# Folding a state scaling into its update, and turning one score matmul round, in a hybrid decoder step

## The chip, the cores and the metric

The kernel runs on one core of a Trainium2 chip. The metric is the device time of one execution in microseconds (us); lower is better. The engines named below are TensorE (PE, with its weight loads PEld), VectorE (DVE), ScalarE (ACT), GpSimd (POOL) and SyncE (SP), which issues most of the transfers.

## The reference

One inference step of one decoder layer, for a prompt of 512 tokens and for a sample group of 8 sequences with 4 new tokens each, with shared weights. Two parts matter here.

The sample group's mLSTM carries a state C (value x key, 128 x 128) for each of 8 sequences b and 4 heads h. With one chunk of 4 tokens the new state is

```python
m_new = jnp.maximum(btot + m, jnp.max(dec, axis=1))
w_s = jnp.exp(dec - m_new[:, None, :])
w_c = jnp.exp(btot + m - m_new)
C_new = w_c[..., None, None] * C + jnp.einsum('bsh,bshe,bshd->bhed', w_s, vi, ki)
```

The prompt's compressed attention compares each of 8 query heads (4 for each of 2 key heads) with 32 compressed key blocks:

```python
s_c = jnp.einsum('bkgqd,bkcd->bkgqc', qi, kc) - slopes * d_c
p_c = masked_softmax(s_c, d_c >= 0)
o_c = jnp.einsum('bkgqc,bkcd->bkgqd', p_c, vc)
```

Everything is float32; the large matmuls are made of three products of split halves.

## The kernel before

The layer is written as Python generators that yield after each small step. `weave(bg, fg)` runs a background generator and lets a foreground one advance in proportion to the numbers that both yield. The stretch that matters is the two `weave(compress(kv), fg)` calls. The background, `compress(kv)`, is the sample group's key and value compression: 8 sequences of 4 steps each, every step a gathered tile turned on VectorE (L1193), summed on GpSimd (L1195), split into two halves on ScalarE and VectorE (L213, L214), and multiplied on TensorE (L218 to L220 into the banks `bd` and `xa`). At the end of a sequence, a tile `cur` is copied to `nxt` with one row's shift by two transfers (L1301, L1302), which line L1330 then reads. The foreground is a chain: the prompt's mLSTM (`mlstm`), with the prompt's compressed scores (`cmp_prompt`, called `cb`) advanced on every second step, then the sample's mLSTM (`mlstm_s`), then the sample's attention (`sample`), which can't begin before `compress(1)` has its weights.

The order written so is only a priority. A planner with a model of the engines' timing then fixes the order of instructions on each engine and each transfer queue, so an edit can move instructions that it doesn't touch. Every queue runs in its order: an instruction that waits holds up what stands behind it. `tc.issue_after` and `tc.keep_in_program_order` pin a few places.

Matmul results go to 8 PSUM banks: `ptp` has two of them ("tp" in the profile), `psp` and `ppo` one each ("sp", "po"). A float32 matmul shows as two records for each call.

In `cmp_prompt`, `kb` holds 32 keys of each key head v, laid out twice along the 128 partitions. For each block i of 128 query tokens, 8 matmuls (L1359) load a 128 x 128 slice of the queries `Q2` as weights and stream the 32 keys; the result has queries on the partitions. Two VectorE adds (L1362) bring in the bias `CB`, and a softmax over 32 keys follows on VectorE, GpSimd and ScalarE (L1366 to L1375). The probabilities are turned back by two transposes (L1382).

In `mlstm_s`, the state lies in two tiles `C0[c]`, each of 4 sequences by 4 heads by 128. Once TensorE has read a tile (transposes L1058, products L1065), GpSimd multiplies all of it by the factors `wcb` (L1070, two instructions of 128 x 2048). Then `outer(h, kz)` makes the outer products of 4 sequences in one PSUM bank (L1100) and VectorE adds that bank to the state (L1101, 8 instructions of 128 x 512). The state goes out in 8 transfers (L1118).

The tile `vcn` (128 x 1024) is a scratch space before it is a result: `compress` loads a quarter of its first-layer weights into it (`vr`, L588), for the keys at the beginning and for the values again after `mlstm` is done in program order (in `produce`, at the earliest).

Of the kernel before, what the change touches and what calls it, by code (L numbers as in the profile page):

```python
# [6 lines left out]
F32 = mybir.dt.float32  # L7
# [3 lines left out]
AF = mybir.ActivationFunctionType  # L11
OP = mybir.AluOpType
# [24 lines left out]
def body(tc, I, O, stage=99, dbg=None):  # L37
    nc = tc.nc
    with ExitStack() as top:
        def pool(name, bufs=1, side="left", stack=None, space=None):  # L40
            kw = dict(name=name, bufs=bufs)
            if space is not None:
                kw["space"] = space
            else:
                kw["side"] = side
                kw["reuse_waits"] = "tile"
            return (stack or top).enter_context(tc.tile_pool(**kw))

        ptp = pool("ptp", 2, space=PSUM)
        psp = pool("psp", 1, space=PSUM)  # L50
# [6 lines left out]
        def bank(p):  # L57
            if p is pxb:
                return rot(pxa, pxc)
            return p.tile([128, 512], F32, name=p_names[id(p)])  # L60
# [4 lines left out]
        def rot(*pools):  # L65
            key = tuple(id(p) for p in pools)
            turn[key] = turn.get(key, -1) + 1
            return bank(pools[turn[key] % len(pools)])
# [8 lines left out]
        def push(name, **kw):  # L77
            st = ExitStack()
            right[name] = st
            return pool(name, stack=st, **kw)  # L80
# [28 lines left out]
        Q2 = qp.tile([128, 8, 512], R32, name="Q2")  # L109
# [41 lines left out]
        ident = const.tile([128, 128], F32, name="ident")  # L151
# [51 lines left out]
        def evac(out, in_, scale=None):  # L203
            flip[0] = (flip[0] + 1) % flip[1]
            if flip[0]:
                nc.scalar.activation(out, in_, AF.Copy, scale=1.0 if scale is None else scale)
            elif scale is None:
                nc.vector.tensor_copy(out, in_)
            else:
                nc.vector.tensor_scalar(out, in_, scale, None, op0=OP.mult)  # L210
# [180 lines left out]
        for c in range(3):  # L391
            c0 = 512 + 264 * c
            dense_N(w0 if c == 0 else w12(c), 264,
                    lambda i, c=c: [((kvn[:, i] if i < 4 else kvs)[:, c * 264:c * 264 + 264], 0, 264)], (pbd, pxb))
# [167 lines left out]
        p = bank(ptp)  # L562
# [170 lines left out]
        vcn = cs.tile([128, 8, 128], F32, name="vcn")  # L733
# [10 lines left out]
        def need(x):  # L744
            while x not in done:
                yield 1
# [201 lines left out]
        def mlstm_s():  # L948
            mw = push("mls", side="right")
            C0 = [mw.tile([128, 4, 4, 128], F32, name=f"C0{c}") for c in range(2)]  # L950
            for b in range(8):
# [13 lines left out]
                                    op=OP.subtract)  # L965
# [23 lines left out]
            p = bank(ptp)  # L989
# [24 lines left out]
            p = bank(ptp)  # L1014
# [6 lines left out]
            p = bank(ptp)  # L1021
            for h in range(4):
                nc.tensor.matmul(p[:, 8 * h:8 * h + 8], sel[:, h], wc, start=True, stop=True)
            wcb = mw.tile([128, 8, 4], F32, name="wcb")
            nc.vector.tensor_copy(wcb.rearrange("p b h -> p h b"), p[:, :32].rearrange("p (h b) -> p h b", h=4))
            p = bank(psp)
# [7 lines left out]
            p = bank(ptp)  # L1034
# [16 lines left out]
            for c in range(5):  # L1051
                if c < 4:
                    CT = CTs[c] = mw.tile([128, 8, 129], F32, name="CT", bufs=2)
                    nc.vector.tensor_copy(CT[:, :, 128], n0T[:, 8 * c:8 * c + 8])
                    for b in (2 * c, 2 * c + 1):
                        p = bank(ptp)
                        for h in range(4):
                            nc.tensor.transpose(p[:, 128 * h:128 * h + 128], C0[b // 4][:, b % 4, h], ident)  # L1058
                        q = 4 * (b % 2)
                        evac(CT[:, q:q + 4, 0:128], p.rearrange("p (h e) -> p h e", h=4))  # L1060
                if c > 0:
                    CT = CTs.pop(c - 1)
                    for b in (2 * c - 2, 2 * c - 1):
                        for h in range(4):
                            nc.tensor.matmul(pn[32 * h:32 * h + 32, 0:129], Qz[:, h, 32 * b:32 * b + 32],  # L1065
                                             CT[:, 4 * (b % 2) + h], start=False, stop=b == 7)
                if c == 2 or c == 4:
                    cc = C0[c // 2 - 1]
                    b0 = 2 * c - 4
                    nc.gpsimd.tensor_tensor(cc, cc, wcb[:, b0:b0 + 4, :, None].to_broadcast([128, 4, 4, 128]), op=OP.mult)  # L1070
                yield
            pe_ = bank(psp)
            for h in range(4):
# [15 lines left out]
            p = bank(psp)  # L1089
            for h in range(4):  # L1090
# [3 lines left out]
                                               op0=OP.mult, op1=OP.add)  # L1094
            nc.sync.dma_start(O[S_N][0].rearrange("b h d -> b (h d)"), nsn)

            def outer(h, kz):
                for c in range(2):
                    p = bank(ptp)
                    nc.tensor.matmul(p, W3[:, h], kz[:, 4 * c:4 * c + 4], start=True, stop=True)  # L1100
                    nc.vector.tensor_tensor(C0[c][:, :, h], C0[c][:, :, h], p.rearrange("p (b d) -> p b d", b=4), op=OP.add)  # L1101

            kzs = {}
            for h in range(5):
# [7 lines left out]
            p = bank(ptp)  # L1112
            nc.tensor.transpose(p[:, :128], hs_, ident)
            for h in range(4):
                nc.vector.scalar_tensor_tensor(oF[:, 4 + h, 512:], p[:, 32 * h:32 * h + 32], gm[:, h:h + 1], sgs[:, h],
                                               op0=OP.mult, op1=OP.mult)
# [224 lines left out]
        def cmp_prompt():  # L1341
            yield from need(("p", 0))
            pk_ = push("cmps", side="right")
            with tc.issue_after(cgs["ml"]["pool"].ins):
                CB = cmp_consts(pk_)
            kb = pk_.tile([128, 2, 32], F32, name="kb")
            for v in range(2):
                for w in range(2):
                    nc.vector.tensor_copy(kb[64 * w:64 * w + 64, v], kcP[64 * v:64 * v + 64])
            yield  # L1350
            pend = {}
            for i in range(5):
                if i < 4:
                    sb = pk_.tile([128, 8, 32], F32, name="csb", bufs=2)
                    S = bank(psp)
                    for j in range(4):
                        for v in range(2):
                            c0 = j * 64 + v * 32
                            nc.tensor.matmul(S[:, c0:c0 + 32], Q2[:, 4 * v + j, 128 * i:128 * i + 128].bitcast(F32), kb[:, v],  # L1359
                                             start=True, stop=True)  # L1360
                    for v in range(2):
                        nc.vector.tensor_tensor(sb[:, 4 * v:4 * v + 4],  # L1362
                                                S[:, :256].rearrange("p (h v s) -> p v h s", h=4, v=2)[:, v],
                                                CB[:, i, 4 * v:4 * v + 4], op=OP.add)
                    mn = pk_.tile([128, 8], F32, name="cmn", bufs=2)
                    nc.vector.tensor_reduce(mn, sb, axis=AX.X, op=OP.min)  # L1366
                    nc.vector.tensor_scalar(mn, mn, 0.1 * BIG, None, op0=OP.min)
                    nc.gpsimd.tensor_tensor(sb, sb, mn[:, :, None].to_broadcast([128, 8, 32]), op=OP.subtract)
                    nc.scalar.activation(sb, sb, AF.Exp, scale=-1.0)
                    sm_ = pk_.tile([128, 8], F32, name="csm", bufs=2)  # L1370
                    nc.vector.tensor_reduce(sm_, sb, axis=AX.X, op=OP.add)
                    nc.vector.tensor_scalar(sm_, sm_, 1e-30, None, op0=OP.max)
                    nc.vector.reciprocal(sm_, sm_)
                    nc.vector.tensor_tensor(sm_, gat[:, i, 0:24:3], sm_, op=OP.mult)
                    nc.gpsimd.tensor_tensor(sb, sb, sm_[:, :, None].to_broadcast([128, 8, 32]), op=OP.mult)  # L1375
                    pend[i] = sb
                    yield
                if i > 0:
                    sb = pend.pop(i - 1)
                    p = bank(ptp)  # L1380
                    for v in range(2):
                        nc.tensor.transpose(p[:, 128 * v:128 * v + 128], sb[:, 4 * v:4 * v + 4], ident)  # L1382
                    nc.scalar.activation(PcT[:, :, 128 * i - 128:128 * i], p[:, :256].rearrange("p (v t) -> p v t", v=2), AF.Copy)
                yield
# [413 lines left out]
        def front():  # L1798
            cb = cgs["cb"] = cmp_prompt()
            n = 0  # L1800
            for x in mlstm():
                yield x
                n += 1
                if ("p", 0) in done and n % 2 == 0:
                    next(cb, None)

        fg = chain(paced(front(), 1.3), paced(mlstm_s(), 2), paced(sample(), .8), open_late())
        flip[1] = 4
        burst(fg, 8)
# [131 lines left out]
        for i in range(2):  # L1941
            x = cw.tile([128, D], F32, name="PTx", bufs=2)
# [365 lines left out]
        for kind, i in order:  # L2308
# [5 lines left out]
            else:  # L2314
                c0, m = parts[i]
# [238 lines left out]
        for hf in (1, 0):  # L2554
            for j in range(8):
                p = rot(*dbk)
# [24 lines left out]
```

## Time and profile before

| | |
|---|---|
| time, median of 3 runs | 1245.95 us (1245.32 to 1247.04) |
| the profiled execution, its own time | 1257.88 us |
| its span in the profile | 1256.2 us |
| granted TensorE clock, mean | 0.97 |
| TensorE matmul, busy | 1174.9 us (94%) |
| VectorE, busy | 867.2 us (69%) |
| ScalarE, busy | 628.6 us (50%) |
| GpSimd, busy | 583.9 us (46%) |

The profile shows one execution. Times in it count from the start of the span. Busy shares are means over stages that differ much; what matters is the stretch in which the changed lines run, from about 290 to 430 us. A matmul's end is modelled, and back-to-back records overlap, so a run of records is best read by its first start and last end.

### The profile page before, as it was taken

The page shows a single profiled execution, that of the slowest core. Times are in us where ns is not written, and L with a number is a line of the kernel's source. Part 1 is how long each engine was busy: PE and PEld are TensorE (multiplying, and loading weights), DVE is VectorE, ACT ScalarE, POOL GpSimd, SP SyncE. Part 2 cuts the span into 40 slices and gives each one's busy share as a digit, 9 for nine tenths or more (in the row PEclk, how much of TensorE's full clock was granted, in tenths as well). Part 3 has the DMA queues.
Part 4 walks back from the last instruction along what each step waited for, and adds up shares of the span by engine and source line. Part 5 has one row for each costly group of instructions (what it writes and reads, how often), then busy time and mean ns, then how long its engine had stood idle before and what let it go on. Part 6 is the DMA issues. An engine that isn't in the chain of part 4 may idle for free.

```text
span 1256.2 us, 24868 instructions
## 1 busy us (share of the span) xinstructions
PE 1174.9 (94%) x9388; PEld 1078.2 (86%) x9388; DVE 867.2 (69%) x1881; ACT 628.6 (50%) x1424; POOL 583.9 (46%) x696
## 2 busy tenths in 40 slices
PE   7999999889998779998989998999999999999996
PEld 5998999588986677876889987589899999999996
DVE  6336674577886876776556576544988878888874
ACT  5235666755546525567533333433565555465452
POOL 1013354577664854744234100034786486486443
PEclk9999999899888899999989999999999999999998
DMA  7324240132142464567659399750023322422411
GB/s 231 100 53 105 83 151 3 52 115 76 59 133 92 124 212 147 174 208 236 160 156 179 101 217 280 258 168 1 1 92 108 104 93 79 133 93 77 135 52 72
DMA packets 141771, 154.33 MB, mean 123 GB/s; under 512 B 17449, under 2 KB 123689, under 8 KB 141394
## 3 DMA queue, kind: packets, MB, share of 16 engines
q1 hardware_dynamic: 131922, 119.17, 31.9%
q0 software_dynamic: 9728, 33.56, 8.3%
q8 instruction: 74, 1.21, 0.4%
q14 instruction: 47, 0.39, 0.1%
HBM read 141.67 MB, written 13.12 MB: 123 GB/s over the span
## 4 chain that ended last, share of the span: by engine, by line
PE 72%; DVE 12%; issue 5%; DMA 3%; ACT 3%; POOL 2%; SPq 2%; another core or an unknown queue 0%; DVEq 0%; POOLq 0%; ACTq 0%
PE bd L218 7%; PE bd L220 7%; PE xc L2255 7%; PE xa L2255 7%; PE bd L219 6%; PE bd L2255 5%; PE tp L2255 5%; PE xa L219 2%; PE xa L218 2%; PE xa L220 2%; DVE sp L2195 2%; PE tp L634 1%; PE xc L219 1%; PE xc L218 1%; PE xc L220 1%
## 5 line engine op out<-in xcount | busy, mean ns | idle before, releaser
L214 POOL TENSOR_TENSOR al<-fraw,ah 128x512 fp32r<-128x512 f32 (+1 forms) x104 | 127.3, 1226 | 152.7 <-ACT ah L213 124.2
L214 DVE TENSOR_TENSOR wlo<-wraw,whi 128x1024 fp32r<-128x1024 f32 (+3 forms) x74 | 76.4, 1061 | 27.6 <-ACT whi L213 27.4
L213 ACT ACTIVATE whi<-wraw 128x1024 fp32r<-128x1024 f32 (+3 forms) x74 | 62.9, 890 | 64.7 <-DMA wraw<-in_w_xv 28.8
L218 PE MATMUL bd<-w1h,xh 128*128 128x256 f32 x256 | 78.8, 309 | 6.6 <-ACT xh L213 5.1
L213 ACT ACTIVATE ah<-fraw 128x512 fp32r<-128x512 f32 (+1 forms) x112 | 65.8, 593 | 37.8 <-PE xc L2255 11.7
L220 PE MATMUL bd<-w1h,xl 128*128 128x256 f32 x256 | 78.7, 313 | 6.3 <-DVE xl L214 6.3
L213 ACT ACTIVATE xh<-xf 128x768 fp32r<-128x768 f32 x64 | 53.5, 842 | 52.6 <-POOL xf L1195 30.7
L1195 POOL TENSOR_TENSOR xf<-xf 128x256 f32<-128x256 f32 x64 | 52.9, 834 | 56.6 <-DVE xf L1193 38.0
L219 PE MATMUL bd<-w1l,xh 128*128 128x256 f32 x256 | 76.1, 298 | 0.0
L214 DVE TENSOR_TENSOR xl<-xf,xh 128x768 fp32r<-128x768 f32 x64 | 62.9, 987 | 15.1 <-ACT xh L213 13.7
L625 POOL TENSOR_SCALAR sb<-sb,rs,gat 128x128 f32<-128x128 f32 (+3 forms) x64 | 45.9, 722 | 54.3 <-DVE rs L624 40.2
L218 PEld LDWEIGHTS bd<-w1h,xh 128*128 128x128 f32 x256 | 51.9, 203 | 11.2 <-ACT xh L213 7.1
L213 ACT ACTIVATE ah<-sp 128x512 fp32r<-128x512 f32 (+1 forms) x64 | 35.5, 555 | 50.3 <-DVE sp L2195 26.6
L220 PEld LDWEIGHTS bd<-w1h,xl 128*128 128x128 f32 x256 | 51.2, 202 | 10.6 <-DVE xl L214 7.6
L219 PEld LDWEIGHTS bd<-w1l,xh 128*128 128x128 f32 x256 | 52.0, 203 | 1.4 <-issue 0.9
L219 PE MATMUL bd<-hlo,whi 128*128 128x272 f32 x176 | 52.0, 296 | 0.0
L218 PE MATMUL bd<-hhi,whi 128*128 128x272 f32 x176 | 51.7, 294 | 0.0
L220 PE MATMUL bd<-hhi,wlo 128*128 128x272 f32 x176 | 51.4, 292 | 0.0
L2195 DVE TENSOR_TENSOR sp<-fraw 128x512 f32<-128x512 f32 (+1 forms) x32 | 47.9, 1497 | 0.2
L214 DVE TENSOR_TENSOR al<-sp,ah 128x512 fp32r<-128x512 f32 (+1 forms) x64 | 40.8, 637 | 9.7 <-ACT ah L213 8.5
L1869 POOL TENSOR_TENSOR acc<-acc,sq 128x272 f32<-128x272 f32 x35 | 31.3, 895 | 34.3 <-ACT sq L1868 33.9
L220 PE MATMUL bd<-hh,wlo 128*128 128x272 f32 x160 | 46.6, 292 | 0.0
(998 smaller groups left out, 4830.4 us busy)
## 6 DMA issues: line engine op xcount, KB each, us to landing
fraw<-in_w_gate SPq DMA_DIRECT2D x11, 1024.0 KB
fraw<-in_w_up SPq DMA_DIRECT2D x11, 1024.0 KB
fraw<-in_w_down SPq DMA_DIRECT2D x24, 384.0 KB
mkv<-in_cache_mem_k SPq DMA_DIRECT2D x64, 128.0 KB
mkv<-in_cache_mem_v SPq DMA_DIRECT2D x16, 512.0 KB
wraw<-in_w_in SPq DMA_DIRECT2D x8, 512.0 KB
wraw<-in_w_xq SPq DMA_DIRECT2D x4, 1024.0 KB
wraw<-in_w_xk SPq DMA_DIRECT2D x4, 1024.0 KB
```

The costliest lines, as they stand in the source:

```text
L213: nc.scalar.activation(hi, src, AF.Copy)
L214: (eng or nc.gpsimd).tensor_tensor(lo, src, hi, op=OP.subtract)
L218: nc.tensor.matmul(out, ah, bh, start=first, stop=False, **kw)
L219: nc.tensor.matmul(out, ah, bl, start=False, stop=False, **kw)
L220: nc.tensor.matmul(out, al, bh, start=False, stop=last, **kw)
L625: (nc.vector, nc.gpsimd)[1].tensor_scalar(sb[:, :n], sb[:, :n], rs, gat[:, i, 3 * h + 1 + br:3 * h + 2 + br], op0=OP.mult, op1=OP.mult)
L634: ins = nc.tensor.transpose(p[:, 128 * k:128 * k + 128], sb[:, 128 * k:128 * k + 128], ident)
L1195: nc.gpsimd.tensor_tensor(xf[:, :, 128:192], xf[:, :, 0:64], xf[:, :, 64:128], op=OP.add)
L1869: nc.gpsimd.tensor_tensor(acc[hf], acc[hf], sq, op=OP.add)
L2195: nc.vector.tensor_tensor(o, a, b, op=op)
L2255: nc.tensor.matmul(p[:, :HALF], w[a][:, k], x[b_][:, k], start=first and k == 0 and i == 0, stop=last and k == n - 1 and i == 2, skip_grou ...
```

## The change

Two edits that don't touch each other.

The sample's state: the two GpSimd multiplications are gone. In `outer`, each of the 8 additions of a bank to the state becomes 4 VectorE instructions, one for each sequence b, that compute state times its factor plus the product (`scalar_tensor_tensor`, 128 x 128, factor read as one value per partition, product read from PSUM): 32 instructions in all.

The prompt's compressed scores: the keys become the weights (32 columns) and all 512 query tokens are streamed past them. For each key head v, the 4 query heads j go to the 4 groups of 32 PSUM partitions of one bank, and ScalarE copies that bank to SBUF, into a view `ST` of the tile `vcn`. In the loop over i, two TensorE transposes bring 128 tokens into the old layout, and one VectorE add over all 8 heads takes the place of two. The generator yields once more.

```diff
@@ mlstm_s
-                if c == 2 or c == 4:
-                    cc = C0[c // 2 - 1]
-                    b0 = 2 * c - 4
-                    nc.gpsimd.tensor_tensor(cc, cc, wcb[:, b0:b0 + 4, :, None].to_broadcast([128, 4, 4, 128]), op=OP.mult)
                 yield
@@ outer
                     nc.tensor.matmul(p, W3[:, h], kz[:, 4 * c:4 * c + 4], start=True, stop=True)
-                    nc.vector.tensor_tensor(C0[c][:, :, h], C0[c][:, :, h], p.rearrange("p (b d) -> p b d", b=4), op=OP.add)
+                    for b in range(4):
+                        x = C0[c][:, b, h]
+                        nc.vector.scalar_tensor_tensor(x, x, wcb[:, 4 * c + b, h:h + 1], p[:, 128 * b:128 * b + 128],
+                                                       op0=OP.mult, op1=OP.add)
@@ cmp_prompt
             pend = {}
+            ST = vcn.rearrange("p (v c) o -> p v (c o)", v=2)
+            for v in range(2):
+                S = bank(psp)
+                for j in range(4):
+                    nc.tensor.matmul(S[32 * j:32 * j + 32], kb[:, v], Q2[:, 4 * v + j].bitcast(F32), start=True, stop=True)
+                nc.scalar.activation(ST[:, v], S, AF.Copy)
+            yield
             for i in range(5):
                 if i < 4:
                     sb = pk_.tile([128, 8, 32], F32, name="csb", bufs=2)
                     S = bank(psp)
-                    for j in range(4):
-                        for v in range(2):
-                            c0 = j * 64 + v * 32
-                            nc.tensor.matmul(S[:, c0:c0 + 32], Q2[:, 4 * v + j, 128 * i:128 * i + 128].bitcast(F32), kb[:, v],
-                                             start=True, stop=True)
                     for v in range(2):
-                        nc.vector.tensor_tensor(sb[:, 4 * v:4 * v + 4],
-                                                S[:, :256].rearrange("p (h v s) -> p v h s", h=4, v=2)[:, v],
-                                                CB[:, i, 4 * v:4 * v + 4], op=OP.add)
+                        nc.tensor.transpose(S[:, 128 * v:128 * v + 128], ST[:, v, 128 * i:128 * i + 128], ident)
+                    nc.vector.tensor_tensor(sb, S[:, :256].rearrange("p (h s) -> p h s", h=8), CB[:, i], op=OP.add)
```

## Rows read from the trace of the kernel before

**Rows 1.** Stretches of 20 us: busy us of each engine, granted clock, DMA.
```profile
320.00:340.00 20.00, 20.00 (x163) 19.11 (x162) 17.66 (x39) 12.88 (x33) 13.65 (x15) 0.91 0.20 60
...
400.00:420.00 20.00, 14.97 (x111) 12.37 (x112) 18.45 (x24) 12.10 (x30) 16.68 (x11) 0.80 0.20 61
```

**Rows 2.** Chain of work that ended last, 280 to 460 us: start, us, what.
```profile
316.00 3.05 PE sp L1359 x16
...
348.70 1.71 PE sp L1359 x16
...
355.05 0.59 PE sp L1359 x6
...
412.48 3.48 DVE dns L1078
```

**Rows 3.** Timeline around the two GpSimd multiplications: start, us, engine.
```profile
395.11 3.61 POOL L1070 TENSOR_TENSOR C<-C,wcb 128x2048 f32<-128x2048 f32 x1 [5.26 <-PE tp L1058]
...
396.55 3.25 DVE L214 TENSOR_TENSOR w1l<-wr,w1h 128x1024 fp32r<-128x1024 f32 x1
...
407.28 1.23 DVE L214 TENSOR_TENSOR w1l<-wr,w1h 128x1024 fp32r<-128x1024 f32 x1 [1.39 <-ACT w1h L213]
...
411.34 4.60 POOL L1070 TENSOR_TENSOR C<-C,wcb 128x2048 f32<-128x2048 f32 x1
...
412.40 3.56 DVE L1078 TENSOR_TENSOR dns<-dns 128x1 f32<-128x1 f32 x1
...
415.91 1.27 POOL L214 TENSOR_TENSOR wsl<-wr,wsh 128x512 fp32r<-128x512 f32 x1
...
416.51 0.64 DVE L1101 TENSOR_TENSOR C<-C,tp 128x512 f32<-128x512 f32 x1
417.08 0.14 DVE L1079 RECIPROCAL dns<-dns 128x1 f32<-128x1 f32 x1
...
417.21 0.79 PE L1100 MATMUL tp<-kz,W 96*128 96x512 f32 x1 [3.67 <-DVE C L1101]
```

**Rows 4.** Groups by line and shape, 308 to 360 us: count, busy us, mean ns.
```profile
L1359 PE MATMUL sp<-kb,Q 128*128 128x32 f32 x64 | 8.9, 292 | 1.4 <-DVE csb L1362 1.1 <-issue 0.2
...
L1362 DVE TENSOR_TENSOR csb<-sp,CB 128x128 f32<-128x128 f32 x8 | 1.9, 279 | 0.9 <-PE sp L1359 0.9
```

**Rows 5.** Timeline, stand-ins for the new TensorE and ScalarE work: start, us, engine.
```profile
353.80 0.41 PE L1382 MATMUL tp<-ident,csb 128*128 128x128 f32 x2
...
408.27 0.43 PE L1065 MATMUL po<-CT,Qz 128*32 128x129 f32 x8
...
463.13 0.58 ACT L206 ACTIVATE kt<-tp 128x512 f32<-128x512 f32 x1
...
602.71 1.07 PE L1522 MATMUL sp<-kt,Qn 128*32 128x512 f32 x8
```

**Rows 6.** Loads into vcn on SP's queue, a copy to nxt, and their readers.
```profile
L588 SPq DMA_DIRECT2D vcn<-in_cmp_w_v x4: 529/546/551, 251.5 to 259.7; - x4
...
347.84 0.53 SPq L1301 DMA_DIRECT2D nxt<-cur  x1
...
409.64 1.06 ACT L213 ACTIVATE w1h<-vcn 128x1024 fp32r<-128x1024 f32 x1 [0.65 <-PE bd L220]
```

**Rows 7.** Durations min/median/max ns, first and last start, of VectorE's state additions and a look-alike.
```profile
L1101 DVE TENSOR_TENSOR C<-C,tp x8: 643/681/690, 409.2 to 425.8; 128x512 f32<-128x512 f32 x8
...
L1093 DVE SCALAR_TENSOR_TENSOR nsn<-n,wN,sp x4: 327/331/334, 385.8 to 399.7; 8x128 f32<-8x128 f32 x4
```

**Rows 8.** Timeline, back-to-back VectorE instructions of one line.
```profile
419.55 1.27 DVE L1101 TENSOR_TENSOR C<-C,tp 128x512 f32<-128x512 f32 x2
...
429.98 0.72 DVE L1115 SCALAR_TENSOR_TENSOR oF<-tp,cv,sgs 128x32 f32<-128x32 f32 x4
```

**Rows 9.** Chain of work, one float32 matmul of 512 columns (two records).
```profile
284.55 0.86 PE tp L799 x2
```

**Rows 10.** The 4 us after 416 us, columns as in rows 1.
```profile
416.00:420.00 4.00, 2.79 (x12) 2.70 (x13) 3.96 (x8) 1.96 (x8) 4.00 (x3) 0.50 0.12 33
```

## The prediction

> **What bounds the kernel now.** I read the page first: TensorE is busy for 94% of the span (the table above), so the question is whether the changed lines run where TensorE sets the pace. The table of 20 us stretches [rows 1] shows two different answers. From 320 to 340 us TensorE is busy all 20 us, with VectorE close behind at 17.66; there a shorter matmul list should shorten the kernel until VectorE takes over. From 400 to 420 us TensorE is busy only 14.97 us and VectorE 18.45; there VectorE sets the pace, and TensorE time is worth little.
>
> Next I read the chain of work that ended last [rows 2]. The score matmuls of L1359 stand in it five times, from 316.00 to 355.05 us; the five pieces add up to 6.3 us (3.05 + 1.71 + 0.59 + 0.37 + 0.59; the middle two of the small ones are not shown). Further on it holds one piece of 3.48 us on a VectorE instruction that handles one number per partition. That is far too long for such an instruction, and the timeline around the GpSimd multiplications explains it [rows 3]. The first multiplication runs from 395.11 to 398.72 us. A VectorE split that starts at 396.55 takes 3.25 us, where the next of the same shape takes 1.23. The second runs from 411.34 to 415.94 us; the tiny L1078 starts at 412.40 and ends at 415.96, at the same moment, where the equally small L1079 takes 0.14. So these two GpSimd instructions hold VectorE, and TensorE then sits idle for 3.67 us until VectorE has freed a bank.
>
> **The scores, part by part.** Removed: 64 records of L1359, 8.9 us of TensorE [rows 4]. The first 16 of them end just before TensorE stalls for other reasons and are not in the chain, so 6.3 us are on the path [rows 2].
>
> Added on TensorE: two runs of 4 calls with 32-column weights and 512 streamed columns. The nearest row is the sample's score matmul of exactly that form, 8 records in 1.07 us [rows 5]; two are 2.1 us. Then 4 pairs of transposes, each like the pair of L1382 at 0.41 us [rows 5]: 1.6 us. TensorE saves 8.9 - 3.7 = 5.2 us.
>
> On the path the first pair of runs takes the place of the block that was off it, about as long, so nothing changes there. Each later block becomes a pair of transposes: -6.3 + 1.6 = -4.7 us. VectorE has 2.3 us of slack in each 20 us of that stretch [rows 1], and the stretch is 40 us long, so 4.6 us is about all that it lets through. The hand-over is new too: bank `psp` is single, and the second run must wait until ScalarE has copied the first out. Such a copy takes 0.58 us [rows 5], and ScalarE is busy for 12.88 of 20 us [rows 1], so some of that shows. I take -3.5 us. Bounds: nothing gained if VectorE already paces the stretch, -5.2 if all TensorE time counts.
>
> Two VectorE adds of 0.28 us [rows 4] become one of twice the width for each i; I count that at nothing. The extra yield moves the foreground chain one step later; it is hidden by the chain's own wait, since the sample's attention can't start before `compress(1)` has its weights. Without that cover it would cost about one step's share of the weave, which the planner's freedom blurs anyway, and I leave it to the range.
>
> Moved: the tile `vcn` now holds the scores. The four loads of the value weights into it were issued from 251.5 to 259.7 us [rows 6], long before the scores. They now have to wait until the last scores have been turned, near where L1359 ends today (355 us [rows 2]). Their reader starts at 409.64 us [rows 6], so some 50 us are left for four loads of 0.55 us of queue time each: nothing, as long as they don't stand in front of something urgent on SP's queue. That is a rival below.
>
> **The state, part by part.** Removed: 8.2 us of GpSimd, which alone is worth nothing, and the hold on VectorE: 3.25 - 1.23 = 2.0 us and 3.56 - 0.14 = 3.4 us, together -5.4 us [rows 3].
>
> Added: 8 additions go, 32 narrower instructions come. The look-alike is L1093, the same operation with one operand in PSUM and 128 elements, 0.331 us; an addition of 512 takes 0.681 [rows 7]. By durations that is 32 x 0.331 - 8 x 0.681 = 10.6 - 5.4 = +5.1 us. Back to back, instructions overlap a little: two additions take 1.27 us, so a second one costs 0.59; four 32-wide ones take 0.72, or 0.18 each [rows 8]. Between these, 128 elements cost about 0.25 us (an estimate by a straight line), and the sum is 32 x 0.25 - 8 x 0.59 = +3.3 us. I take +4.0, between the two, since the four of one bank run back to back and then wait for the next.
>
> Would GpSimd's other work hold the new instructions as well? The addition at 416.51 us, with one operand in PSUM, took 0.64 us under a GpSimd split that ran from 415.91 to 417.18 [rows 3], so I take it that it doesn't. Net: -5.4 + 4.0 = -1.4 us. Bounds: -5.4 if the additions hide in VectorE's gaps, +5.1 if the holds were not on the path.
>
> [...]
>
> **The sum.** -3.5 - 1.4 = -4.9 us on the profiled execution's own 1257.88 us, that is 1253.0, or 0.39% less. The median of the runs shown is 1245.95, nearly 1% below the profiled one; the same share of it gives 1241.1 us. A difference of 0.2%, 2.5 us, is about what a measurement of this kernel can tell from no change, so "faster" is below 1243.5 and "slower" above 1248.4.
>
> **The rivals.** First, nothing arrives, because VectorE paces both places. For it: 17.66 and 18.45 of 20 us [rows 1]. The TensorE gain becomes waiting for VectorE (0), and the state costs its durations' sum (-5.4 + 5.1 = -0.3): about 1245.6 us. Against it: TensorE shows no idle time at all from 320 to 340 us.
>
> Second, the change does not do what it says, if the four calls into the four partition groups run one after the other: a call of 512 columns alone takes 0.86 us [rows 9], 8 of them 6.9 instead of 2.1. Then -4.9 + 4.8 = -0.1: 1245.9 us. Against it: L1065, written in a plain loop over the groups like the new code, gets 8 records of 129 columns into 0.43 us [rows 5].
>
> Third, more than counted. [...] If the holds go and the new instructions fit in VectorE's gaps, the state gives all of its -5.4, the scores -5.2: -10.6, or 1235.4 us.
>
> Fourth, slower: the loads into `vcn` block SP's queue. That queue works in order, and the copies of `cur` to `nxt` stand on it, one at 347.84 us [rows 6], in the middle of the score blocks. If the planner's model expects the scores to be done sooner than they are, it puts a load in front of such a copy. That copy then waits until the last turn, about 355.5 us, some 8 us; L1330, then the transposes of its result, then TensorE's queue wait for it. The price is up to 8 us: -4.9 + 8 = +3.1, or 1249.0 us. It decides from a hold of 4.9 us (no change) and shows as slower from 7.4 us. Against it: the planner has some 50 us in which to place them, and it needs none of them early.
>
> **How the numbers follow.** The forecast 0.50, more than counted 0.12, VectorE paces 0.18, groups in turn 0.04, blocked queue 0.16. Faster: 0.62; within 0.2%: 0.22; slower: 0.16. The planner reorders instructions that the edit doesn't touch, which may shift any of these by a microsecond or two. The likeliest case's own range is 1238 to 1243.5 us. The range for 8 in 10 reaches to the case of more than counted below (1235) and a little past the blocked queue above (1249.5).
>
> **What would show each step.** Right: the score runs take about 1 us each, eight records overlapping, and the chain holds no long piece on the new score lines; from 320 to 340 us TensorE has gaps or the stretch is shorter. No VectorE instruction of a few elements takes 3 us between 390 and 420; the 32 new instructions have a mean of about 0.33 us and VectorE's busy time grows by about 5 - 5.4 us, so hardly at all, while GpSimd's falls by 8. The transfers to S_C start earlier than today. Wrong: waits of TensorE for ScalarE's copy of the score bank; a long wait on SP's queue at the loads of `vcn` with a copy to `nxt` behind it; VectorE busy without a gap from 400 to 432 us with TensorE waiting for the state's banks. The prediction falls if the kernel is more than 2.5 us slower with none of these, which would mean that the planner's new order decides.

## The result, and the profile after

The changed kernel took 1239.63 us (median of 14 runs) beside 1247.51 us for the kernel before (14 runs). The ratio is 0.9939, with an interval from 0.9923 to 0.9956: about 7.6 us less, where 4.9 were forecast. A few executions of these kernels took 1600 us or more; the ratios leave them out. The profiled execution of after took 1238.97 us, close to its median. That of before, with 1257.88 us, lay 10 us above its own, so the difference of the two traces (18.9 us) is more than the change is worth. The experiments therefore start with a second profile of the kernel before.

The page of after, its first part (busy us, share of the span, instructions):

```profile
span 1237.3 us, 24816 instructions
## 1 busy us (share of the span) xinstructions
PE 1165.2 (94%) x9348; PEld 1066.7 (86%) x9348; DVE 845.1 (68%) x1901; ACT 632.1 (51%) x1426; POOL 580.1 (47%) x694
```

The stretches of 20 us that answer to [rows 1], and two beside them, with the same columns:

```profile
320.00:340.00 20.00, 20.00 (x177) 19.41 (x177) 17.05 (x36) 13.35 (x34) 14.21 (x16) 1.00 0.27 76
340.00:360.00 20.00, 18.29 (x157) 17.12 (x156) 16.51 (x36) 8.02 (x16) 14.20 (x15) 1.00 0.49 151
...
400.00:420.00 20.00, 17.46 (x165) 14.45 (x165) 17.17 (x25) 13.68 (x27) 16.59 (x14) 0.83 0.20 61
420.00:440.00 20.00, 16.20 (x92) 14.28 (x91) 18.33 (x53) 8.95 (x26) 8.94 (x11) 0.74 0.54 155
```

From 400 to 420 us TensorE is busy for 17.46 us instead of 14.97. The new lines come from the view of single lines (count, duration min/median/max in ns, first and last start); their numbers are those of the changed file, where L1096, L1099, L1074 and L1215 were L1100, L1101, L1078 and L1216:

```profile
L1355 PE MATMUL sp<-Q,kb x16: 592/604/617, 310.1 to 312.9; 128*32 128x512 f32 x16
L1356 ACT ACTIVATE vcn<-sp x2: 594/596/598, 311.3 to 315.9; 128x512 f32<-128x512 f32 x2
L1363 PE MATMUL sp<-ident,vcn x8: 270/272/278, 319.6 to 351.7; 128*128 128x128 f32 x8
L1364 DVE TENSOR_TENSOR csb<-sp,CB x4: 382/406/412, 320.6 to 360.2; 128x256 f32<-128x256 f32 x4
L1099 DVE SCALAR_TENSOR_TENSOR C<-C,wcb,tp x32: 299/336/343, 416.9 to 432.9; 128x128 f32<-128x128 f32 x32
L588 SPq DMA_DIRECT2D vcn<-in_cmp_w_v x4: 538/571/607, 345.8 to 352.5; - x4
```

The loads into `vcn` moved from 251.5 to 345.8 us [rows 6], as the text said. The timelines of VectorE and of GpSimd, which answer to [rows 3] (no multiplication is left):

```profile
419.44 2.28 DVE L1074 TENSOR_TENSOR dns<-dns 128x1 f32<-128x1 f32 x1 [0.76 <-ACT dns L1073]
421.64 0.85 DVE L1099 SCALAR_TENSOR_TENSOR C<-C,wcb,tp 128x128 f32<-128x128 f32 x3
```

```profile
419.40 0.76 POOL L1194 TENSOR_TENSOR xf<-xf 128x256 f32<-128x256 f32 x1
420.10 1.29 POOL L214 TENSOR_TENSOR wsl<-po,wsh 128x512 fp32r<-128x512 f32 x1
421.31 0.35 POOL L1153 MEMSET hidt<- 128x288 f32 x1
```

The tiny L1074 is still held, now behind the short GpSimd instructions shown: 2.28 us in place of 3.56. And the waits of TensorE from 390 to 480 us (total, times, longest):

```profile
PE tp L1096 <- DVE C L1099: 2.6, 2, 2.4
PE bd L218 <- ACT xh L213: 2.5, 1, 2.5
PE tp L1035 <- issue: 1.5, 1, 1.5
```

No hole of TensorE is longer than 2.5 us here. Before had one of 3.67 [rows 3].

### The profile page after: what moved, and what is told of

It is laid out like the page before. It is cut to its first block, busy times and chain, and to the rows that moved or that the text cites. A ratio compares the mean times of both kernels' runs of the same rounds, so it can differ in the third digit from the quotient of the medians.

```text
span 1237.3 us, 24816 instructions
## 1 busy us (share of the span) xinstructions
PE 1165.2 (94%) x9348; PEld 1066.7 (86%) x9348; DVE 845.1 (68%) x1901; ACT 632.1 (51%) x1426; POOL 580.1 (47%) x694
## 4 chain that ended last, share of the span: by engine, by line
PE 72%; DVE 9%; DMA 5%; issue 5%; POOL 3%; ACT 3%; SPq 2%; DVEq 0%; POOLq 0%; ACTq 0%
PE xa L2255 8%; PE xc L2255 8%; PE bd L218 6%; PE bd L220 6%; PE bd L219 6%; PE bd L2255 6%; PE tp L2255 6%; PE xa L218 2%; PE xa L220 2%; PE xa L219 2%; PE tp L634 1%; DMA wraw<-in_w_xv 1%; PE xc L219 1%; DMA wraw<-in_w_out 1%; PE xc L220 1%
## 5 line engine op out<-in xcount | busy, mean ns | idle before, releaser
L214 DVE TENSOR_TENSOR wlo<-wraw,whi 128x1024 fp32r<-128x1024 f32 (+3 forms) x74 | 76.5, 1062 | 29.5 <-ACT whi L213 29.3
L218 PE MATMUL bd<-w1h,xh 128*128 128x256 f32 x256 | 77.9, 306 | 6.3 <-ACT xh L213 4.3
L220 PE MATMUL bd<-w1h,xl 128*128 128x256 f32 x256 | 77.4, 306 | 3.5 <-DVE xl L214 3.5
L218 PEld LDWEIGHTS bd<-w1h,xh 128*128 128x128 f32 x256 | 50.4, 197 | 12.3 <-ACT xh L213 6.2
L220 PEld LDWEIGHTS bd<-w1h,xl 128*128 128x128 f32 x256 | 49.7, 196 | 7.7 <-DVE xl L214 4.7
L213 ACT ACTIVATE ah<-sp 128x512 fp32r<-128x512 f32 (+1 forms) x64 | 35.7, 557 | 38.2 <-PE xc L2255 14.7
L218 PE MATMUL bd<-hhi,whi 128*128 128x272 f32 x176 | 52.1, 296 | 0.0
L220 PE MATMUL bd<-hhi,wlo 128*128 128x272 f32 x176 | 51.8, 294 | 0.0
L213 ACT ACTIVATE ah<-po 128x512 fp32r<-128x512 f32 (+1 forms) x64 | 35.7, 558 | 23.6 <-PE xa L2255 14.1
L220 PE MATMUL bd<-hh,wlo 128*128 128x272 f32 x160 | 46.6, 292 | 0.0
```

The lines of the kernel that those rows point to most:

```text
L213: nc.scalar.activation(hi, src, AF.Copy)
L214: (eng or nc.gpsimd).tensor_tensor(lo, src, hi, op=OP.subtract)
L218: nc.tensor.matmul(out, ah, bh, start=first, stop=False, **kw)
L220: nc.tensor.matmul(out, al, bh, start=False, stop=last, **kw)
```

## The experiments

The change has three parts: the scores, the state, and the extra `yield` (below: the step). Each ratio below is to runs of the kernel before on the same chip (medians 1258.67, 1254.63 and 1254.89 us in three sets; the kernel before itself thus differs by 4 us between them, and lies 7 to 11 us above the result's 1247.51). The table has all eight combinations, and from each profile the stretch between the third and the last copy of `cur` to `nxt`: its length, the idle time of TensorE in it (length less busy time), the mean granted clock, and VectorE's wait before its copy to `vcP` near 460 us. Outside that stretch the profiled executions differ by a few us only, but for scores + step, which loses 8 us more behind it.

| kernel | ratio (95%) | length | idle | clock | wait at vcP |
|---|---|---|---|---|---|
| before again | 1.0002 (0.9979 to 1.0025) | 262.95 | 29.2 | 0.91 | 5.4 |
| step | 0.9910 (0.9882 to 0.9938) | 248.70 | 23.9 | 0.95 | none |
| scores | 0.9970 (0.9953 to 0.9988) | 253.74 | 29.3 | 0.93 | 3.8 |
| scores + step | 1.0063 (1.0041 to 1.0086) | 257.55 | 34.4 | 0.91 | 5.0 |
| state | 0.9931 (0.9906 to 0.9957) | 255.82 | 25.9 | 0.93 | 3.8 |
| state + step | 0.9994 (0.9978 to 1.0010) | 257.32 | 31.0 | 0.92 | 3.7 |
| scores + state | 0.9921 (0.9899 to 0.9943) | 249.85 | 25.6 | 0.93 | 3.6 |
| all (the change) | 0.9896 (0.9870 to 0.9923) | 242.90 | 21.1 | 0.94 | none |

**The kernel before, again.** No edit.

> The kernel before, unchanged, profiled a second time, as a control. Its first profiled execution took 1257.88 us, 10 us above the median of all its runs. If that was one slow execution, this profile lies near 1247 us, and comparing it with the first by stretches shows where the 10 us were lost. Theory 1 (local gains): the two places keep what they had in the first profile, a score list of 64 records and 8.9 us on TensorE and two VectorE instructions of 3 us and more next to the GpSimd multiplications. Theory 2 (the gain read in the traces is largely chance of the first profile): the copies of cur to nxt come 10 us or more earlier than in the first profile, near their places in the changed kernel. Ratio to before: 1.000, within 0.002.

Measured: 1.0002; the profiled execution took 1262.84 us. The `nxt` copies lie within 4 us of the first profile's, so those 10 us were no slow place in it but the pace of these executions (the median of before in this set is 1258.67 us). Its windows view gives the whole stretch, and below it are the timelines of GpSimd, VectorE and TensorE around the second multiplication:

```profile
311.81:574.76 262.95, 233.79 (x1925) 202.08 (x1925) 196.86 (x422) 134.91 (x284) 155.84 (x170) 0.91 0.46 145
```

```profile
409.85 3.62 POOL L1070 TENSOR_TENSOR C<-C,wcb 128x2048 f32<-128x2048 f32 x1
413.42 1.27 POOL L214 TENSOR_TENSOR wsl<-wr,wsh 128x512 fp32r<-128x512 f32 x1
414.64 1.26 POOL L1135 TENSOR_TENSOR wr<-wr 128x512 f32<-128x512 f32 x1
```

```profile
409.63 0.69 DVE L1101 TENSOR_TENSOR C<-C,tp 128x512 f32<-128x512 f32 x1 [1.97 <-PE po L1065]
410.24 6.49 DVE L214 TENSOR_TENSOR xl<-xf,xh 128x768 fp32r<-128x768 f32 x1
...
416.65 1.21 DVE L214 TENSOR_TENSOR w1l<-vcn,w1h 128x1024 fp32r<-128x1024 f32 x1
417.78 0.15 DVE L1078 TENSOR_TENSOR dns<-dns 128x1 f32<-128x1 f32 x1
```

```profile
416.78 0.58 PE L220 MATMUL bd<-w1h,xl 128*128 128x256 f32 x1 [5.33 <-DVE xl L214]
```

This time the multiplication met a split of 0.95 us and not the tiny L1078. Two more GpSimd instructions followed the multiplication without a pause, to 415.90 us; the split took 6.49 us and ended 0.83 us after them, and TensorE stood idle for 5.33 us. So in these two profiles the price of the hold was set by what it met and, in this one, by what GpSimd had queued behind it. A queue behind it does not always lengthen the hold: in the first profile L1078 ended at 415.96, just after GpSimd's next instruction had begun at 415.91 [rows 3]. Of two VectorE instructions under this multiplication one was held and one was not: the split, with both inputs in SBUF, for 5.5 us; L1101, with one input in PSUM, starts at 409.63, is under the multiplication from 409.85, and takes 0.69 us, its usual time (0.643 to 0.690 in [rows 7]). What makes the difference no run shows.

**The scores with the step.** All of the diff in `cmp_prompt`; the state as before.

> The kernel before with the scores' part of the change alone (keys stationary, turned, one more step of the foreground); the state is scaled on GpSimd as before. Prediction's term: -3.5 us of 1247.5, a ratio of 0.9972. Rival 1 (VectorE paces the stretch from 320 to 340 us): 0 us, ratio 1.000. Rival 3 (order: the foreground starts one step later and the background gets ahead): more than the term, about -6 us, ratio 0.995, with the nxt copies earlier by 10 us or more from 370 us on, as in the changed kernel.

Measured: 1.0063, slower, which none of the theories expected. Up to 404 us its `nxt` copies are those of the changed kernel (403.72 beside 403.66); then it loses what it had. Its waits of TensorE from 390 to 480 us:

```profile
PE tp L1100 <- DVE C L1101: 5.1, 2, 4.8
PE xc L1216 <- DVE vcP L1268: 4.2, 1, 4.2
```

and the two instructions behind the first of them, on GpSimd and on VectorE:

```profile
423.48 3.62 POOL L1070 TENSOR_TENSOR C<-C,wcb 128x2048 f32<-128x2048 f32 x1
```

```profile
425.46 2.03 DVE L1152 TENSOR_SCALAR w<-w 128x128 f32<-128x128 f32 x1 [3.73 <-DMA w<-in_cmp_w_v]
427.42 0.67 DVE L1101 TENSOR_TENSOR C<-C,tp 128x512 f32<-128x512 f32 x1
```

VectorE stood at L1152 for 3.73 us, waiting for its load, and was then held there by the second multiplication: 2.03 us, where the same line takes 0.23 in the run of state + step. L1101, which frees TensorE's bank, was queued behind it.

**The state.** The rest of the diff: multiplications out, fused updates in.

> The kernel before with the state's part of the change alone (no GpSimd multiplications, 32 narrow fused updates on VectorE). Prediction's term: -1.4 us, ratio 0.9989. Rival (the holds cost more than their 5.4 us, since TensorE stands idle and its granted clock falls behind them): -4 to -5.4 us, ratio 0.996. Rival (VectorE paces): 0. By any of them the nxt copies up to 390 us stay where they were and those after 420 us come earlier by the gain.

Measured: 0.9931, 8.7 us of 1258.67. The term of -1.4 is out in this order; the rival that the holds cost more is right in direction and too low.

**The step.** One line more, no instruction more:

```diff
             pend = {}
+            yield
             for i in range(5):
```

> The kernel before with nothing but one more step of the foreground ahead of the score blocks: every instruction the same, only their order may differ. Prediction: nothing, 1.000 within 0.002. Rival (order): the foreground comes one step later, the background's matmuls run ahead and fill TensorE where it stood idle; then a part of the gain of 7.6 us appears here, ratio 0.998 or less.

Measured: 0.9910. The step that was costed at nothing gives more here than the whole change did in the result (0.9939), and as much as it gives below (0.9896) within the intervals. The copies to `nxt` come 14.7 us earlier at 375 us (389.92 to 375.19) and stay so: the background runs ahead while the foreground is later (the last transposes of the state start at 418.3 instead of 404.8 us).

**After, again.** No edit.

> The changed kernel, unchanged, beside the others of this call. On the chip of the first four experiments the kernel before took 1258.7 us and its copies of cur to nxt came where the first profile had them, so the 10 us above the median in that profile are the chip's and not a slow place. Theory A (the change is worth 7.6 us on any chip): ratio 0.994, within 0.002. Theory B (the value depends on which chip's pace decides the meetings of GpSimd and TensorE): the ratio moves towards 0.985 on a chip on which the kernel before takes 1258 us.

Measured: 0.9896. The interval leaves out theory A's 0.994 and does not reach theory B's 0.985; at 0.9923 it just meets the interval of the result. The value of the change is itself 0.6 to 1.0%, by the set of runs.

**State and step.** The state's part of the diff and the one line of the step.

> The kernel before with the state's part and the extra step of the foreground, and the scores as they were. Alone, the step gave -0.90% and the state -0.69%. Theory 1 (each part's gain is its own, they add): -1.6%, ratio 0.984, which beats the changed kernel. Theory 2 (both gains are the same one: each only shifts VectorE, TensorE and the GpSimd transfers so that the wait of 4 to 5 us at the copy to vcP near 470 us goes away or shrinks): no more than the better of them, -0.9%, ratio 0.991. Read it from that wait: below 0.5 us here by both.

Measured: 0.9994; together the two best single parts give nothing. Neither theory allowed that: the wait at `vcP` is there (3.7 us), and TensorE has a new hole, the longest shown here:

```profile
PE bd L218 <- ACT xeh L213: 8.0, 1, 8.0
PE bd L218 <- ACT xh L213: 3.9, 1, 3.9
PE xc L1215 <- DVE vcP L1267: 3.1, 1, 3.1
```

**The scores without the step.** The new scores, less this line:

```diff
                 nc.scalar.activation(ST[:, v], S, AF.Copy)
-            yield
             for i in range(5):
```

> The kernel before with the scores' part alone and without the extra step of the foreground. With the step it was 0.63% slower. Theory 1 (the scores' own work is worth -3.5 us, and what went wrong in that run was the meeting at the copy to vcP and the two GpSimd multiplications): 0.997 if that wait is away, near 1.002 if it is there. Theory 2 (the new scores themselves cost): slower again, 1.006.

Measured: 0.9970, or -3.8 us; the forecast term was -3.5, and the interval leaves out the rival by which nothing arrives. It came although the wait at `vcP` is 3.8 us, so theory 1's condition was wrong. It came also with the two holes that scores + step has, somewhat shorter:

```profile
PE tp L1100 <- DVE C L1101: 4.6, 2, 4.3
PE xc L1216 <- DVE vcP L1268: 3.2, 1, 3.2
```

**The scores kept in `PcT`.** The loads of the value weights are free again:

```diff
-            ST = vcn.rearrange("p (v c) o -> p v (c o)", v=2)
+            ST = PcT
```

> The changed kernel with the scores kept in PcT instead of vcn (same size, written chunk by chunk behind the turns that read it), so that the four loads of the value weights into vcn are free to go early again, as in the kernel before. Prediction: the moved loads cost nothing, so the same time as the changed kernel within 0.2%. Rival 4 (the loads stand in front of something urgent on SP's queue): faster than the changed kernel by up to 8 us, 0.65%. Order theory: the loads' new place alone shifts the meetings, and the time moves by several us in either direction while TensorE's work stays the same.

Measured: 0.9885 (0.9863 to 0.9908), the same as the change within the intervals, with the loads back at 250.9 us:

```profile
L588 SPq DMA_DIRECT2D vcn<-in_cmp_w_v x4: 529/540/552, 250.9 to 259.2; - x4
```

The moved loads cost nothing that can be measured; the blocked queue is out. In the profile of the change SP's queue stood at them for 2.1 us, and the copy behind them then waited for its own data. This is also the one edit that the planner met with the order of the change: the two traces list TensorE's, ScalarE's and GpSimd's instructions in the same order, and VectorE's but for one.

**Scores and state without the step.** The same line taken out of the changed kernel.

> The changed kernel without the extra step of the foreground, that is both parts of the work and the old order of steps; it completes the table of the eight combinations. Theory A (the parts' own work decides: scores -0.30%, state -0.69% alone): ratio 0.990, the same as the changed kernel, 0.9896. Theory B (what decides is whether TensorE's signal reaches VectorE's copy to vcP in time near 470 us, and the other holes of TensorE between 390 and 480 us): 0.990 if that wait is below 0.5 us, 0.994 or more if it is 4 to 5 us as in the six kernels that showed it.

Measured: 0.9921, with a wait at `vcP` of 3.6 us. The interval holds the numbers of both theories, so this run alone decides nothing; it completes the table.

**No scaling at all.** The kernel before without its multiplications; the state is left unscaled.

```diff
-                if c == 2 or c == 4:
-                    cc = C0[c // 2 - 1]
-                    b0 = 2 * c - 4
-                    nc.gpsimd.tensor_tensor(cc, cc, wcb[:, b0:b0 + 4, :, None].to_broadcast([128, 4, 4, 128]), op=OP.mult)
```

> The kernel before with the two GpSimd multiplications left out and nothing in their place, so the state is not scaled. Prediction's term: their hold on VectorE is worth -5.4 us, ratio 0.9957; TensorE's hole of 5.3 us behind the second one is gone. Rival (the hold costs more, since TensorE's granted clock falls behind the hole): -8 us or more, 0.9935. Rival (order): the parts meet in another way, and the ratio lies nearer to 1 or below 0.991, with holes of TensorE that have nothing to do with the state.

Measured: 0.9931 (0.9910 to 0.9951), or 8.7 us, exactly what the state's edit gave with its 32 instructions. The hole of 5.3 us is gone, the stretch has 21.6 us idle instead of 29.2, and the clock is 0.94 instead of 0.91:

```profile
310.89:559.33 248.44, 226.81 (x1924) 195.96 (x1924) 191.09 (x422) 134.87 (x283) 149.53 (x168) 0.94 0.48 153
```

The number is the one of the rival with the clock. That the holds alone cost it is not shown: from 403 us on the planner also gave TensorE and the other engines another order, so 8.7 us is the price of the multiplications and of the order that comes with them. The 32 updates cost nothing that shows; as each of the two intervals reaches about 3 us to either side, the difference is known to about 4 us, and the forecast +4.0 lies at the edge of that.

**Plain additions in the changed kernel.** The state is left unscaled.

```diff
-                    for b in range(4):
-                        x = C0[c][:, b, h]
-                        nc.vector.scalar_tensor_tensor(x, x, wcb[:, 4 * c + b, h:h + 1], p[:, 128 * b:128 * b + 128],
-                                                       op0=OP.mult, op1=OP.add)
+                    nc.vector.tensor_tensor(C0[c][:, :, h], C0[c][:, :, h], p.rearrange("p (b d) -> p b d", b=4), op=OP.add)
```

> The changed kernel with 8 plain additions of 512 elements in place of the 32 fused updates of 128, so the state is not scaled anywhere. Prediction's term: the 32 fused updates cost 4.0 us of VectorE more than the 8 additions (3.3 to 5.1), so without them the kernel would be 4 us faster than the changed one if VectorE's time counts there, ratio to before 0.9864 against 0.9896. Rival (VectorE's updates hide: between 416 and 433 us TensorE waited for them only 2.6 us in 2): no more than 2.6 us, 0.9875 or above.

Measured: 1.0042 (1.0019 to 1.0065), 1.5% slower than the change with less work in it. Where the time went can't be read: its only profile spans 1612.6 us. Both theories expected it faster than the change. The run has a second reading, since the same kernel is scores + step without its multiplications. That one had 1.0063 (1.0041 to 1.0086), so the removal that gave 8.7 us above gives 2.6 us here, with intervals that overlap. In neither pair is the order of the other engines' instructions kept, so the price of the holds by themselves stays open.

**Value gathers on SP's queue.** Other rows of the cache are fetched than the page table names.

```diff
+            if kv == 1:
+                src = I["cache_v_cmp"][0].rearrange("n (c t) v d -> (n c) (t v d)", t=4)
+                nc.sync.dma_start(cgs[kv, b][:, 512 * q:512 * q + 512], src[128 * q:128 * q + 128])
+                return
```

> The kernel before with the 32 indirect transfers of the compressed value cache (GpSimd) replaced by plain transfers of the same size on SP's queue, which fetch other rows than the page table names. Of ten profiled kernels, six show VectorE waiting 3.7 to 5.4 us before its copy to vcP for a signal of TensorE whose matmuls had been recorded as ended; in all six GpSimd issues four value gathers and one key gather without a pause around it, in the other four the key gather comes 2 us later. Theory G (the run of five indirect issues or their landing holds the signal): no such wait here, below 0.5 us. Rival (it is the copy's or the matmuls' own): 4 to 5 us again. The time itself is left open, since SP's queue gets 32 transfers more: 0.985 to 1.01.

Measured: 0.9882, as much as the whole change, with a wait at `vcP` of 0.5 us for a matmul that had just ended, as theory G has it. TensorE's order is another one here too. Its row in the waits of VectorE from 440 to 480 us:

```profile
DVE vcP L1272 <- PE xc L1266: 0.5, 1, 0.5
```

## Why the prediction was right, and where it was too small

**The direction and the scores.** TensorE's list was sized rightly. In the second profile of before, L1359 takes 7.8 us (8.9 in [rows 4]); after, the runs and turns take 3.6:

```profile
L1359 PE MATMUL sp<-kb,Q 128*128 128x32 f32 x64 | 7.8, 271 | 1.3 <-DVE csb L1362 1.1 <-issue 0.2
L1355 PE MATMUL sp<-Q,kb 128*32 128x512 f32 x16 | 2.1, 604 | 0.0
L1363 PE MATMUL sp<-ident,vcn 128*128 128x128 f32 x8 | 1.5, 273 | 0.0
```

The four groups run side by side: 16 records of 604 ns start within 2.8 us, and the rival of groups in turn is out. The scores alone gave -3.8 us; that this is so near the term of -3.5 is luck, as the table shows below. Gaps of TensorE from 320 to 340 us, one of the two signs set for that stretch, did not come (20.00 us busy before and after); they come from 340 to 360 us, where it is busy 18.29 us and the second profile of before has 20.00. Two other signs failed: the transfers of the new state start later (429.2 us, before 425.9), and GpSimd's busy time fell by 4 us, not by 8.

**The state: the term that was mis-sized.** It was put at -1.4 us and measured -8.7 in the old order. The hold was taken as the two long VectorE instructions of one profile, -5.4. Without the multiplications the kernel before gives 8.7: in the second profile the hold went on while GpSimd's next instructions ran (6.49 us), TensorE's hole is about as long as the hold, and without them the granted clock of the stretch is 0.94 instead of 0.91. In the first profile the clock is 0.50 over the 4 us from 416 us on, around and behind the end of the 3.67 us hole [rows 3, rows 10]; there L218 to L220 start every 0.21 us, against 0.12 in the 1.5 us ahead of the hole, at 1.00. In the first profile of after those 4 us have 1.00. How much of the 8.7 is the hold and how much the new order is not shown; beside scores + step the same removal gives 2.6 us, within the noise. And of the +4.0 for VectorE's narrow updates nothing showed, to within about 4 us: they have 336 ns, as the look-alike said, but TensorE waited for them only 2.6 us in all. That none of them is held by GpSimd was right (343 ns at most).

**The step, "counted at nothing".** This failed most. The forecast left "a microsecond or two" to the planner's order; the step alone moved the time by -0.9%, and with the state in place by +0.6% in the table (0.9931 to 0.9994). It has no price of its own: by the four pairs of the table it is -0.92, +0.63, +0.93 and -0.25%, the last within its intervals. The scores change sign too (-0.32, +1.53, -0.10, -0.98; mean near 0). Only the state gains in three of its four pairs (-0.71, -0.49, -1.67, and +0.84 with the step), with a mean of -0.5%.

**What the order does.** The time of a variant is that of the stretch from 311 to some 560 us, and there it is TensorE's list, plus its holes, plus a lower clock. By TensorE's idle time in that stretch the eight variants fall into the order of their ratios, but for one, before again, whose 29.2 us are less than those of the two variants ahead of it (29.3 and 31.0). From before again to the change again the profiled stretch shortens by 20.0 us (the two executions lie 20.5 us apart, more than the 13 us of the medians): 8.1 idle and 12.0 busy. Of the busy time the scores are 4.2. The clock covers the other 7.8: 0.09 of 262.95 us is lost to it before, 0.06 of 242.90 after, which is 9 us less (an estimate from two rounded means). Here is the row of the change's first profile, beside the one of before above:

```profile
311.00:552.46 241.46, 220.99 (x1884) 189.28 (x1881) 191.76 (x442) 134.46 (x285) 150.77 (x168) 0.94 0.50 159
```

That the change as a whole gives 7.6 us is measured. How much of it the two work edits give is not: without the step they give 0.9921, but beside the step alone (0.9910) the whole change (0.9896) can't be told apart. Why the parts do not add is shown only as far as the idle time goes. The holes lie at other places in each variant and have other causes, 8.0 us in state + step the longest shown; but single holes do not rank the variants, since the state alone, at 0.9931, has one of 5.0 us, and the scores without the step, at 0.9970, none above 4.3 from 390 to 480 us. That they come from which foreground step meets which background step is likely and not shown. What order the planner would choose for a given edit was not foreseen by any theory here, and stays open.

So the prediction was right on the direction, with a mechanism that is real in its parts (a shorter list, a hold that is gone), and in part lucky on the size: its terms do not add, and one step of the weave, counted at nothing, moves the time by up to 0.9% either way, where the whole forecast was 0.39%.

**Not settled.** Whether the 32 updates would cost something in the changed kernel, since the plain additions came out slower and left no readable profile; and what the holds cost in an order that stays the same.

## What to carry to other kernels

Price a hold by the row behind it: what GpSimd has queued next, which instruction is caught (L1078 for 3.56 us in one profile here, a split for 6.49 in the other), and TensorE's hole with the clock behind it (3.67 us and 0.50 in the first); one profile shows one meeting only, so take a second before sizing it. Before a difference is called the price of what was taken out, see whether the two traces keep the order of the rest. Where two streams are woven, run an edit of the order alone as a control, since it can be worth more than the work that is saved, and run the parts of a change in all combinations before one of them is given the credit. A variant that beats its neighbours by 1% in such a kernel may owe it to a meeting that did not happen.

## What was not expected of the hardware

Eight of the thirteen readable profiles (all but that of the plain additions) show VectorE idle for 3.6 to 5.4 us before its copy to `vcP`; in both profiles of before, in scores + step and in the state alone the last 3.4 to 4.5 us of it come after the matmuls of that tile are recorded as ended. In the other five the wait is 0.5 us at most; in the first profile of after and in the step alone the copy starts 0.09 us after that end. In the run of scores + step, GpSimd's timeline, then that of TensorE and VectorE:

```profile
462.99 0.95 POOL L573 DMA_INDIRECT cgat<-in_cache_v_cmp,gx  x1 [0.31 <-issue]
464.24 0.95 POOL L573 DMA_INDIRECT cgat<-in_cache_v_cmp,gx  x1 [0.30 <-issue]
465.49 0.95 POOL L573 DMA_INDIRECT cgat<-in_cache_v_cmp,gx  x1 [0.30 <-issue]
466.75 0.95 POOL L573 DMA_INDIRECT gat<-in_cache_k_slc,gx  x1 [0.30 <-issue]
```

```profile
463.69 0.75 PE L1262 MATMUL xc<-w,hid 128*32 128x64 f32 x15
...
464.37 0.66 PE L1513 MATMUL tp<-ident,gat 128*128 128x128 f32 x4
...
468.90 0.29 DVE L1268 COPY vcP<-xc 128x128 f32<-128x128 f32 x1 [4.97 <-remote]
468.96 0.60 ACT L206 ACTIVATE kt<-tp 128x512 f32<-128x512 f32 x1 [5.21 <-remote]
...
469.25 0.47 PE L1216 MATMUL xc<-ident,ys 128*128 128x128 f32 x1 [4.22 <-DVE vcP L1268]
```

The last matmul of L1262 is recorded as ended at 464.44 us; VectorE and ScalarE, which wait for two different ones, go on together at 468.90 and 468.96. In all eight profiles GpSimd issues four value gathers and a key gather with pauses of 0.30 us there. In four of the five without the wait the key gather comes 1.91 us later, as in the run of the step alone:

```profile
459.56 0.94 POOL L573 DMA_INDIRECT cgat<-in_cache_v_cmp,gx  x1 [0.30 <-issue]
462.41 0.94 POOL L573 DMA_INDIRECT gat<-in_cache_k_slc,gx  x1 [1.91 <-PE tp L1513]
```

In the fifth the value gathers are not on GpSimd. So the wait goes with that run of five indirect transfers. Whether and how these hold up TensorE's signal no run shows, and taking the gathers away also changed the order.
